# Places of the moving tiles and weight buffers modulo 512 bytes, and dense products in passes of 256 columns

## Chip, cores and metric

The kernel runs on one core of one Trainium2 chip. The metric is the device time of one execution in microseconds (us): the median of three runs, 2741.3 us before the change. All rows of profiles come from one profiled execution each.

## The reference

A trunk of two layers over 256 tokens of width 2048, float32. Layer 0 has differential attention, layer 1 a gated DeltaNet; each layer ends with a gated feed-forward with a short causal convolution (ConvFFN).

```python
for i in range(DEPTH):
    h = rms_norm(x, mixer_norm[i])
    if i % 2 == 0:
        x = x + diff_attention(h, w_qkv, ..., w_o, lambda_init)
    else:
        x = x + gated_deltanet(h, w_in, conv_w, a_log, dt_bias, norm_g, w_out)
    x = x + conv_ffn(rms_norm(x, ffn_norm[i]), ffn_w_up[i], ffn_conv_w[i], ffn_conv_b[i], ffn_w_down[i])

def conv_ffn(h, w_up, conv_w, conv_b, w_down):
    u = causal_dwconv(h @ w_up, conv_w) + conv_b
    val, gate = jnp.split(u, 2, axis=-1)
    return (jax.nn.silu(gate) * val) @ w_down
```

Nearly all of the arithmetic is in the dense products: q, k, v and w_o of the attention (2048 wide), w_up to 2 x 5504 and w_down back in each feed-forward, w_in, w_z and w_out of the DeltaNet.

## The kernel before

Activations lie transposed: features on the 128 partitions, the 256 tokens along the free axis. `x` is 16 tiles of 256 columns. `self.h` is 16 tiles of 128 x 2 x 256 in float32r; the first half of a tile is the high part of the normed activation, the second half the rest, so that the two add up to the float32 value (`norm_tile`). The feed-forward's own activations are kept in the same form in 43 tiles `ac`, the attention's in 16 tiles `ac`, the DeltaNet's in tiles `oc`.

Weights arrive in chunks of 512 KB: four tiles of 128 rows by 256 columns. `weights` loads one to `raw` (four buffers, SP's queue), ScalarE writes the high part `whi` (line 78) and VectorE the rest `wlo` (line 79), three buffers each.

`dense` makes a block of 256 output features in two PSUM banks, one for each 128. For each row tile k of the weights and each column tile c it issues three products: hi x hi, lo x hi, hi x lo. In the form with `fold` these are three passes of 256 columns into the first half of the bank (lines 107 to 109: a triple). Otherwise one pass of 512 columns takes both parts of the activation at once (line 112), and a pass of 256 columns adds the weight's rest to the second half of the bank (line 115: a pair); the halves are added after, in `merge` (lines 125 and 126) or `add_out` (line 235). Pairs are used for w_qk, w_o, w_gate, both w_up and both w_down but for the last block of the second; triples for w_in, w_out and that block. `dense_tok` (w_v and w_z) has the tokens on the partitions: there the weights are the moving operand, 512 columns wide, and slices of h are loaded into the array (lines 140 to 142).

The order is that of the program: attention, feed-forward, DeltaNet, feed-forward. Within a stage the blocks follow each other; small products of the attention and of the DeltaNet run as generators, one step after each chunk (`tick`). The numbers of passes, from the loops:

| stage | pairs | triples | passes of 512 alone |
|---|---|---|---|
| w_qk, w_gate | 512 + 16 | | |
| w_v, w_z | | | 384 + 768 |
| w_o | 256 | | |
| first w_up, w_down | 1376 + 688 | | |
| w_in, w_out | | 1024 + 512 | |
| second w_up, w_down | 1376 + 602 | 86 | |

Where a tile stands in a partition follows from the sizes of the tiles allocated before it. A tile of h or `ac` has 2048 bytes in each partition, a buffer of `whi` or `wlo` 4096, and the slice of 128 columns that one pass loads into the array 512.

Of the kernel before, what the change touches and what calls it, by code (L numbers as in the profile page):

```python
# [8 lines left out]
F32 = mybir.dt.float32  # L9
F32R = mybir.dt.float32r  # L10
AF = mybir.ActivationFunctionType
ALU = mybir.AluOpType
# [13 lines left out]
class Trunk:  # L26
    """Activations lie transposed, features on the partitions and the 256 tokens along the free axis.

    A float32 operand of a dense product is split into two float32r parts (hi + lo, exact), and
    the passes carry hi * hi, hi * lo and lo * hi; the parts of an activation lie side by side, so  # L30
    that one pass of a weight's hi takes both, and the two halves of the sum are added after. Work that follows a dense block and needs the
    tensor engine again runs as a generator in the background, a step after each chunk of weights.
    """

    def __init__(self, ctx, tc):
# [13 lines left out]
        self.h = [self.cp.tile([P, 2, T], F32R, tag=f"h{k}", name=f"h{k}") for k in range(KD)]  # L49
# [4 lines left out]
        nc.scalar.preload_act_table_set(LNEXP)  # L54

# [11 lines left out]
    def weights(self, ap):  # L67
        """A chunk [128, k, n] of weights, in two parts."""
        nc = self.nc
        nk, n = ap.shape[1:]  # L70

        def tile_(tag, dt, bufs):
            t = self.wp.tile([P, CK * T], dt, tag=tag, name=tag, bufs=bufs)
            return t[:, :nk * n].rearrange("p (k n) -> p k n", n=n)

        raw, hi, lo = tile_("raw", F32, 4), tile_("whi", F32R, 3), tile_("wlo", F32R, 3)
        nc.sync.dma_start(raw, ap)
        nc.scalar.copy(hi, raw)  # L78
        nc.vector.tensor_tensor(lo, raw, hi.bitcast(F32), ALU.subtract)  # L79
# [10 lines left out]
    def dense(self, w, kt, acts, tiles=2, fold=False, lead=0):  # L90
        """out^T of 128 * tiles features, a PSUM bank for each 128, in two halves to be added,
        or (fold) in one, which spares the vector engine the sum."""
        nc = self.nc
        ps = self.banks()
        for k0, nk in self.chunks(kt, CK, lead):
            hi, lo = self.weights(w[:, k0:k0 + nk, :])
            steps = [(k, c) for k in range(nk) for c in range(tiles)]
            if fold and k0 + nk == kt:
                steps = [(k, c) for c in range(tiles) for k in range(nk)]
            for k, c in steps:  # L100
# [3 lines left out]

                def sole():
                    o = ps[:, c, :T]
                    nc.tensor.matmul(o, hi[:, k, s], a[:, 0, :], start=first, stop=False)  # L107
                    nc.tensor.matmul(o, lo[:, k, s], a[:, 0, :], start=False, stop=False)  # L108
                    nc.tensor.matmul(o, hi[:, k, s], a[:, 1, :], start=False, stop=last)  # L109

                def one():
                    nc.tensor.matmul(ps[:, c, :], hi[:, k, s], a, start=first, stop=last)  # L112

                def two():
                    nc.tensor.matmul(ps[:, c, T:], lo[:, k, s], a[:, 0, :], start=False, stop=False)  # L115

                for f in ((sole,) if fold else (one, two) if first else (two, one)):
                    f()
# [3 lines left out]
    def merge(self, ps, u):  # L122
        """The two halves of a dense block, added and divided by the rms of the tokens."""
        nc = self.nc
        nc.scalar.copy(u, ps[:, :, T:])
        nc.vector.tensor_tensor(u, ps[:, :, :T], u, ALU.add)
# [22 lines left out]
    def norm_tile(self, k, gcol):  # L149
        """One tile of x * gain, split; 1 / rms is applied after the products."""  # L150
# [19 lines left out]
    def norm_stat(self, wait=1):  # L170
        """1 / rms of each token, over all partitions and as columns."""
# [22 lines left out]
    def lnexp(self, inst):  # L194
        """After inst, the activations within run from the table set that has both functions."""
# [4 lines left out]
    def conv(self, out, u, taps, bias):  # L200
        """Causal depthwise convolution along the tokens."""
# [10 lines left out]
    def rsqrt(self, out, ps, n):  # L212
        """(ps / n + eps) ** -0.5"""
# [4 lines left out]
    def split(self, out, a):  # L218
        """Two float32r parts of a, out[:, 0] + out[:, 1] = a."""
# [3 lines left out]
    def total(self, out, parts):  # L223
        """Sums over the partitions of tiles, in two parts each, on every partition."""
# [6 lines left out]
    def add_out(self, blk, ps, done, fold=False):  # L231
# [9 lines left out]
    def project(self, w, kt, acts, done, final=False):  # L241
        """x += a projection; with final, the last block is left a tile at a time."""
# [3 lines left out]
        if final:  # L246
            ps = self.dense(w[n - 1], kt, acts, fold=True)
# [5 lines left out]
    def ffn(self, w_up, w_down, nj, cols_ap, done, final=False):  # L253
        """cols_ap: taps (3) and bias, each for the values and the gates, a column for each tile."""
        nc = self.nc
        self.spawn(self.norm_stat())
        with self.tc.tile_pool(name="fp", bufs=1) as fp:
            cols = fp.tile([P, 4, 2, nj], F32, tag="fcols", name="fcols")
            nc.scalar.dma_start(cols, cols_ap)
            acts = []  # L260
            for j in range(nj):
                ps = self.dense(w_up[j], KD, self.h_acts)
                c = []
                u = fp.tile([P, 2, T], F32, tag="u", name="u", bufs=2)
                self.merge(ps, u)
# [8 lines left out]
                ac = fp.tile([P, 2, T], F32R, tag=f"ac{j}", name="ac")  # L274
# [4 lines left out]
    def attention(self, w_qk, w_v, w_o, nh, dist_ap, ident_ap, qg, kg, lvec, sub, start, done, lambda_init):  # L279
        """qg, kg, lvec (4 columns), sub (2 columns): per-partition columns."""  # L280
        nc, mp = self.nc, self.mp
        with self.tc.tile_pool(name="at", bufs=1) as at:
# [5 lines left out]
            dist = at.tile([P, 384], F32, tag="dist", name="dist")  # L288
# [44 lines left out]
            def weigh(h, qn, kn, go, aT):  # L333
                """The differential attention weights of a head, keys on the partitions."""
# [77 lines left out]
    def gdn(self, w_gate, w_in, w_z, w_out, nb, hb, gate_ap, const_ap, hot_ap, conv_col, ng, done):  # L412
        """nb batches of hb query/key heads, each with two value heads; 128 wide, all of them.

        const_ap: identity, mask of the decays, upper triangle of ones.
        All 256 tokens are one chunk: u = (I + strict(K K^T . D) beta)^-1 v, o = (Q K^T . D) beta u, with
        D_ij = exp(G_i - G_j) for i >= j, beta within the exponent. Matrices lie transposed, as
        [second half of the keys: 128 queries | first half: 256 queries].
        """
# [5 lines left out]
        with tc.tile_pool(name="gd", bufs=1) as gd:  # L425
            self.spawn(self.norm_stat())
            con = gd.tile([P, 384], F32, tag="con", name="con")
# [18 lines left out]
            def lin(ps):  # L446
                u = gd.tile([P, 2, T], F32, tag="u", name="u", bufs=2)
                nc.vector.tensor_tensor(u, ps[:, :, :T], self.rstd.unsqueeze(1).to_broadcast([P, 2, T]), ALU.mult)
# [9 lines left out]
            def keys(hq, c, cc, b0, res):  # L458
                """Decayed K K^T and Q K^T of the two value heads of a query/key head."""
# [52 lines left out]
            def invert(cc, lqs, inv):  # L512
                """Inverses of the unit lower triangular 32x32 blocks on the diagonal, one in a partition."""
# [23 lines left out]
            def levels(TT, Ta, lts, ttc, tcc, m0):  # L537
                """Transposes of the inverses of the 128x128 blocks, from those of the 32x32 ones."""
# [54 lines left out]
            def group(gi, gr, lqs, inv, vt, ready, zts, acts):  # L593
                """Outputs of the value heads of a group, on their way to the last projection."""
# [67 lines left out]
            def out(b, acts):  # L662
                for blk in range(KD // 2):
                    ps = self.dense(w_out[b * (KD // 2) + blk], 2 * hb, lambda k: self.await_(acts, k), fold=True)
# [244 lines left out]
```

## Time and profile before

| | |
|---|---|
| runs | 2741.3 us median of 3 (2741.16 to 2741.84) |
| profiled execution | span 2741.9 us, 44249 instructions, clock 0.999 |
| PE busy | 2727.6 us, 17526 passes |
| PEld busy | 2433.3 us |
| DVE busy | 1920.3 us |
| ACT busy | 1498.2 us |
| DMA | 481 MB, mean 175 GB/s |

PE is TensorE's products, PEld its weight loads (they overlap the products), DVE is VectorE, ACT ScalarE, POOL GpSimd, SP the engine that issues the transfers. A pass's duration in a row is from its start until its result is written; the next pass starts long before that, so the rate of the engine is read from the starts of passes that follow each other.

### The profile page before, as it was taken

To read this page: it belongs to the slowest core of one execution; us is meant where nothing else is said; L and a number is where in the kernel's file an instruction comes from. 1 tells how busy PE (TensorE), PEld (TensorE's weight loads), DVE (VectorE), ACT (ScalarE), POOL (GpSimd) and SP (SyncE) were. 2 spreads that over 40 slices of the span, in tenths; PEclk is the share of its full clock that TensorE was granted. 3 is DMA by queue.
4 is the path that set the end of the run, shared out by engine and by line. 5 is a ranking of instruction groups with operands and counts; after the bars stand their busy time and mean duration, and the time that the engine had idled before them with its cause. 6 is when DMAs were issued, how large, how long until landed. Compare 5 with 4: busy or idle time off the path is not lost.

```text
span 2741.9 us, 44249 instructions
## 1 busy us (share of the span) xinstructions
PE 2727.6 (99%) x17526; PEld 2433.3 (89%) x17526; DVE 1920.3 (70%) x2845; ACT 1498.2 (55%) x2094; POOL 117.0 (4%) x220
## 2 busy tenths in 40 slices
PE   8999999999999999999999999999999999999999
PEld 7888888888888888989989989989998888888888
DVE  7776577777777555679687687688677777776444
ACT  6665555555555444574564664574555555554333
POOL 0000000000000000022011011021000000000000
PEclk9999999999999999999999999999999999999999
DMA  6555565555555665655354454454455555556664
GB/s 210 170 166 173 156 193 186 185 186 188 187 185 188 187 187 185 187 158 180 116 164 168 131 170 146 154 167 157 152 185 187 186 186 186 188 187 194 191 195 151
DMA packets 135359, 481.00 MB, mean 175 GB/s; under 512 B 15344, under 2 KB 18416, under 8 KB 135152
## 3 DMA queue, kind: packets, MB, share of 16 engines
q1 hardware_dynamic: 134000, 475.57, 55.0%
q8 instruction: 137, 2.24, 0.3%
q10 hardware_dynamic: 1152, 2.61, 0.3%
q14 instruction: 70, 0.57, 0.1%
HBM read 476.03 MB, written 2.10 MB: 174 GB/s over the span
## 4 chain that ended last, share of the span: by engine, by line
PE 99%; DMA 0%; DVE 0%; ACT 0%; SPq 0%; issue 0%; DVEq 0%
PE ps L112 41%; PE ps L115 21%; PE ps L108 7%; PE ps L107 7%; PE ps L109 7%; PE ps L141 3%; PE ps L140 3%; PE ps L142 3%; PE mp L610 2%; PE mp L228 1%; PE mp L498 1%; PE mp L553 0%; PE mp L562 0%; PE mp L475 0%; PE mp L580 0%; PE mp L574 0%
## 5 line engine op out<-in xcount | busy, mean ns | idle before, releaser
L79 DVE TENSOR_TENSOR wlo<-raw,whi 128x1024 fp32r<-128x1024 f32 (+2 forms) x909 | 1107.1, 1218 | 571.5 <-ACT whi L78 568.7
L78 ACT CAST whi<-raw 128x1024 fp32r<-128x1024 f32 (+2 forms) x909 | 947.0, 1042 | 775.0 <-PE ps L112 475.5
L112 PE MATMUL ps<-h,whi 128*128 128x512 f32 x3280 | 1155.2, 398 | 6.1 <-DVE h L155 6.1
L115 PE MATMUL ps<-h,wlo 128*128 128x256 f32 x3280 | 908.4, 282 | 4.1 <-DVE wlo L79 4.1
L112 PEld LDWEIGHTS ps<-h,whi 128*128 128x128 f32 x3280 | 611.3, 188 | 147.7 <-DVE h L155 6.1
L115 PEld LDWEIGHTS ps<-h,wlo 128*128 128x128 f32 x3280 | 617.5, 188 | 14.1 <-DVE wlo L79 4.7
L112 PE MATMUL ps<-ac,whi 128*128 128x512 f32 x1546 | 543.5, 396 | 0.2 <-DVE x L235 0.2
L115 PE MATMUL ps<-ac,wlo 128*128 128x256 f32 x1546 | 430.2, 281 | 0.0
L112 PEld LDWEIGHTS ps<-ac,whi 128*128 128x128 f32 x1546 | 289.1, 188 | 68.7 <-ACT whi L78 0.5
L115 PEld LDWEIGHTS ps<-ac,wlo 128*128 128x128 f32 x1546 | 290.3, 188 | 2.0
L108 PE MATMUL ps<-h,wlo 128*128 128x256 f32 x1024 | 287.5, 281 | 0.0
L107 PE MATMUL ps<-h,whi 128*128 128x256 f32 x1024 | 286.1, 280 | 0.0
L109 PE MATMUL ps<-h,whi 128*128 128x256 f32 x1024 | 285.9, 279 | 0.0
L108 PEld LDWEIGHTS ps<-h,wlo 128*128 128x128 f32 x1024 | 193.7, 189 | 2.1
L107 PEld LDWEIGHTS ps<-h,whi 128*128 128x128 f32 x1024 | 193.1, 189 | 1.5 <-ACT whi L78 0.2
L109 PEld LDWEIGHTS ps<-h,whi 128*128 128x128 f32 x1024 | 193.2, 189 | 1.0
L140 PE MATMUL ps<-whi,h 128*128 128x512 f32 x384 | 151.5, 395 | 0.0
L141 PE MATMUL ps<-wlo,h 128*128 128x512 f32 x384 | 151.2, 394 | 0.0
L142 PE MATMUL ps<-whi,h 128*128 128x512 f32 x384 | 150.8, 393 | 0.0
L108 PE MATMUL ps<-oc,wlo 128*128 128x256 f32 x512 | 144.2, 282 | 0.0
L107 PE MATMUL ps<-oc,whi 128*128 128x256 f32 x512 | 144.1, 282 | 0.0
L109 PE MATMUL ps<-oc,whi 128*128 128x256 f32 x512 | 143.9, 281 | 0.0
(215 smaller groups left out, 2710.6 us busy)
## 6 DMA issues: line engine op xcount, KB each, us to landing
raw<-w_up SPq DMA_DIRECT2D x344, 512.0 KB, 4.4
raw<-w_down SPq DMA_DIRECT2D x160, 512.0 KB, 3.5
raw<-w_in SPq DMA_DIRECT2D x128, 512.0 KB, 4.4
raw<-w_z SPq DMA_DIRECT2D x64, 512.0 KB, 3.7
raw<-w_out SPq DMA_DIRECT2D x64, 512.0 KB, 3.8
raw<-w_qk SPq DMA_DIRECT2D x63, 512.0 KB, 3.9
raw<-w_v SPq DMA_DIRECT2D x32, 512.0 KB, 3.5
raw<-w_o SPq DMA_DIRECT2D x32, 512.0 KB, 4.7
```

Of the source, the lines that this page charges most:

```text
L78: nc.scalar.copy(hi, raw)
L79: nc.vector.tensor_tensor(lo, raw, hi.bitcast(F32), ALU.subtract)
L107: nc.tensor.matmul(o, hi[:, k, s], a[:, 0, :], start=first, stop=False)
L108: nc.tensor.matmul(o, lo[:, k, s], a[:, 0, :], start=False, stop=False)
L109: nc.tensor.matmul(o, hi[:, k, s], a[:, 1, :], start=False, stop=last)
L112: nc.tensor.matmul(ps[:, c, :], hi[:, k, s], a, start=first, stop=last)
L115: nc.tensor.matmul(ps[:, c, T:], lo[:, k, s], a[:, 0, :], start=False, stop=False)
L140: nc.tensor.matmul(ps[:, c, :], ah, hi[:, k, :], start=first, stop=False)
L141: nc.tensor.matmul(ps[:, c, :], ah, lo[:, k, :], start=False, stop=False)
L142: nc.tensor.matmul(ps[:, c, :], al, hi[:, k, :], start=False, stop=last)
L228: last = self.nc.tensor.matmul(out, self.onesr, p[:, j], start=i + j == 0, stop=i + j == n)
L610: nc.tensor.matmul(p[:, v, :], l(v), r[:, v, :], start=i == 0, stop=i == len(terms) - 1)
```

## The change

Four things, in one diff. First, each tile of h and of the feed-forward's `ac` gets 8 spare columns (32 bytes), so that the next one starts 32 bytes further modulo 512 (`staggered`); `fcols` and `dist` get spare columns as well, which moves what is allocated after them. Second, the three buffers of `whi` and of `wlo` become six tiles with names of their own, with 0, 32, 16 and 16, 56, 0 spare columns; they still take turns in threes. Third, `dense` uses triples everywhere but in the second feed-forward's w_up (`halves`), where the pass of 512 columns stays and the weight's rest now goes to the first half of the bank, after it. `merge` and `add_out` lose the sum of halves where there are none. Fourth, in the last chunk of a block all of column tile 0 is done before column tile 1, in every block and not only in folded ones. Comments are removed too.

```diff
-        self.h = [self.cp.tile([P, 2, T], F32R, tag=f"h{k}", name=f"h{k}") for k in range(KD)]
+        self.h = [self.staggered(self.cp, f"h{k}", f"h{k}") for k in range(KD)]
+        self.nth = 0
...
+    def staggered(self, pool, tag, name):
+        return pool.tile([P, 2 * T + 8], F32R, tag=tag, name=name)[:, :2 * T].rearrange("p (i t) -> p i t", i=2)
...
-        def tile_(tag, dt, bufs):
-            t = self.wp.tile([P, CK * T], dt, tag=tag, name=tag, bufs=bufs)
+        def tile_(tag, dt, bufs, spare=0):
+            t = self.wp.tile([P, CK * T + spare], dt, tag=tag, name=tag, bufs=bufs)
             return t[:, :nk * n].rearrange("p (k n) -> p k n", n=n)
-        raw, hi, lo = tile_("raw", F32, 4), tile_("whi", F32R, 3), tile_("wlo", F32R, 3)
+        b = self.nth % 3
+        self.nth += 1
+        raw = tile_("raw", F32, 4)
+        hi, lo = tile_(f"whi{b}", F32R, 1, (0, 32, 16)[b]), tile_(f"wlo{b}", F32R, 1, (16, 56, 0)[b])
...
-    def dense(self, w, kt, acts, tiles=2, fold=False, lead=0):
+    def dense(self, w, kt, acts, tiles=2, lead=0, halves=False):
...
-            if fold and k0 + nk == kt:
+            if k0 + nk == kt:
                 steps = [(k, c) for c in range(tiles) for k in range(nk)]
...
-                for f in ((sole,) if fold else (one, two) if first else (two, one)):
-                    f()
+                o = ps[:, c, :T]
+                if halves:
+                    nc.tensor.matmul(ps[:, c, :], hi[:, k, s], a, start=first, stop=last)
+                    nc.tensor.matmul(o, lo[:, k, s], a[:, 0, :], start=False, stop=False, skip_group_check=True)
+                    continue
+                nc.tensor.matmul(o, hi[:, k, s], a[:, 0, :], start=first, stop=False)
+                nc.tensor.matmul(o, lo[:, k, s], a[:, 0, :], start=False, stop=False)
+                nc.tensor.matmul(o, hi[:, k, s], a[:, 1, :], start=False, stop=last)
...
     def merge(self, ps, u):
-        nc.scalar.copy(u, ps[:, :, T:])
-        nc.vector.tensor_tensor(u, ps[:, :, :T], u, ALU.add)
-        nc.vector.tensor_tensor(u, u, self.rstd.unsqueeze(1).to_broadcast([P, 2, T]), ALU.mult)
+        self.nc.vector.tensor_tensor(u, ps[:, :, :T], self.rstd.unsqueeze(1).to_broadcast([P, 2, T]), ALU.mult)
...
-        for i in range(1 if fold else 2):
-            self.nc.vector.tensor_tensor(x, ps[:, :, i * T:(i + 1) * T], x, ALU.add)
+        self.nc.vector.tensor_tensor(x, ps[:, :, :T], x, ALU.add)
...
-            cols = fp.tile([P, 4, 2, nj], F32, tag="fcols", name="fcols")
+            cols = fp.tile([P, 8 * nj + 64], F32, tag="fcols", name="fcols")[:, :8 * nj]
+            cols = cols.rearrange("p (t h j) -> p t h j", t=4, h=2)
...
-                ps = self.dense(w_up[j], KD, self.h_acts)
+                ps = self.dense(w_up[j], KD, self.h_acts, halves=final)
...
-                ac = fp.tile([P, 2, T], F32R, tag=f"ac{j}", name="ac")
+                ac = self.staggered(fp, f"ac{j}", "ac")
...
-            dist = at.tile([P, 384], F32, tag="dist", name="dist")
+            dist = at.tile([P, 384 + 72], F32, tag="dist", name="dist")[:, :384]
```

More of the change, by code (lines that the diff above doesn't have):

```diff
@@ L103, in dense @@
                 s = slice(c * P, (c + 1) * P)
[L105 to L115, printed above, removed]
-                for f in ((sole,) if fold else (one, two) if first else (two, one)):
-                    f()
+                o = ps[:, c, :T]
+                if halves:
+                    nc.tensor.matmul(ps[:, c, :], hi[:, k, s], a, start=first, stop=last)
+                    nc.tensor.matmul(o, lo[:, k, s], a[:, 0, :], start=False, stop=False, skip_group_check=True)
[3 more added lines that the diff above has]
+                nc.tensor.matmul(o, hi[:, k, s], a[:, 1, :], start=False, stop=last)
             self.tick()
@@ L122, in merge @@
     def merge(self, ps, u):
-        nc = self.nc
-        nc.scalar.copy(u, ps[:, :, T:])
-        nc.vector.tensor_tensor(u, ps[:, :, :T], u, ALU.add)
-        nc.vector.tensor_tensor(u, u, self.rstd.unsqueeze(1).to_broadcast([P, 2, T]), ALU.mult)
+        self.nc.vector.tensor_tensor(u, ps[:, :, :T], self.rstd.unsqueeze(1).to_broadcast([P, 2, T]), ALU.mult)
     def dense_tok(self, w, kt, acts):
@@ L229, in total, with add_out @@
         return last
-    def add_out(self, blk, ps, done, fold=False):
+    def add_out(self, blk, ps, done):
         x = self.x[:, 2 * blk:2 * blk + 2, :]
-        for i in range(1 if fold else 2):
-            self.nc.vector.tensor_tensor(x, ps[:, :, i * T:(i + 1) * T], x, ALU.add)
+        self.nc.vector.tensor_tensor(x, ps[:, :, :T], x, ALU.add)
         if done:
@@ L246, in project @@
         if final:
-            ps = self.dense(w[n - 1], kt, acts, fold=True)
+            ps = self.dense(w[n - 1], kt, acts)
             for c in range(2):
@@ L261, in ffn @@
             for j in range(nj):
-                ps = self.dense(w_up[j], KD, self.h_acts)
+                ps = self.dense(w_up[j], KD, self.h_acts, halves=final)
                 c = []
                 u = fp.tile([P, 2, T], F32, tag="u", name="u", bufs=2)
-                self.merge(ps, u)
+                if final:
+                    nc.scalar.copy(u, ps[:, :, T:])
+                    nc.vector.tensor_tensor(u, ps[:, :, :T], u, ALU.add)
+                    nc.vector.tensor_tensor(u, u, self.rstd.unsqueeze(1).to_broadcast([P, 2, T]), ALU.mult)
+                else:
+                    self.merge(ps, u)
                 for half in range(2):
@@ L426, in gdn @@
             self.spawn(self.norm_stat())
-            con = gd.tile([P, 384], F32, tag="con", name="con")
+            con = gd.tile([P, 384], F32, tag="con", name="con")[:, :384]
             nc.sync.dma_start(con, const_ap)
@@ L447, in lin @@
                 u = gd.tile([P, 2, T], F32, tag="u", name="u", bufs=2)
-                nc.vector.tensor_tensor(u, ps[:, :, :T], self.rstd.unsqueeze(1).to_broadcast([P, 2, T]), ALU.mult)
+                self.merge(ps, u)
                 return u
@@ L663, in out @@
                 for blk in range(KD // 2):
-                    ps = self.dense(w_out[b * (KD // 2) + blk], 2 * hb, lambda k: self.await_(acts, k), fold=True)
-                    self.add_out(blk, ps, done if b == nb - 1 else None, True)
+                    ps = self.dense(w_out[b * (KD // 2) + blk], 2 * hb, lambda k: self.await_(acts, k))
+                    self.add_out(blk, ps, done if b == nb - 1 else None)
             pg = self.dense(w_gate, KD, self.h_acts, tiles=1)
@@ L679, in gdn @@
                         hq = heads[i]
-                        c = convs(lin(self.dense(w_in[hq * 2], KD, self.h_acts, fold=True)), (hq, nq + hq))
+                        c = convs(lin(self.dense(w_in[hq * 2], KD, self.h_acts)), (hq, nq + hq))
                         self.spawn(keys(hq, c, cc, 2 * i, lqs))
@@ L698, in gdn @@
                         hq = heads[i]
-                        c = convs(lin(self.dense(w_in[hq * 2 + 1], KD, self.h_acts, fold=True)),
+                        c = convs(lin(self.dense(w_in[hq * 2 + 1], KD, self.h_acts)),
                                   (2 * nq + 2 * hq, 2 * nq + 2 * hq + 1))
@@ L714, in gates @@
         lin = gd.tile([P, T], F32, tag="tmp", name="glin", bufs=1)
-        nc.scalar.copy(lin, pg[:, 0, T:])
-        nc.vector.tensor_tensor(lin, pg[:, 0, :T], lin, ALU.add)
-        nc.vector.tensor_tensor(lin, lin, self.rstd, ALU.mult)
+        nc.vector.tensor_tensor(lin, pg[:, 0, :T], self.rstd, ALU.mult)
         yield
```

## The prediction

> **What bounds the kernel now.** I read the page first: busy times, granted clock, chain of waits, costliest groups.
>
> ```profile
> span 2741.9 us, 44249 instructions
> PE 2727.6 (99%) x17526; PEld 2433.3 (89%) x17526; DVE 1920.3 (70%) x2845; ACT 1498.2 (55%) x2094; POOL 117.0 (4%) x220
> PEclk9999999999999999999999999999999999999999
> PE 99%; DMA 0%; DVE 0%; ACT 0%; SPq 0%; issue 0%; DVEq 0%
> L79 DVE TENSOR_TENSOR wlo<-raw,whi 128x1024 fp32r<-128x1024 f32 (+2 forms) x909 | 1107.1, 1218 | 571.5 <-ACT whi L78 568.7
> L78 ACT CAST whi<-raw 128x1024 fp32r<-128x1024 f32 (+2 forms) x909 | 947.0, 1042 | 775.0 <-PE ps L112 475.5
> L108 PE MATMUL ps<-h,wlo 128*128 128x256 f32 x1024 | 287.5, 281 | 0.0
> L107 PE MATMUL ps<-h,whi 128*128 128x256 f32 x1024 | 286.1, 280 | 0.0
> L109 PE MATMUL ps<-h,whi 128*128 128x256 f32 x1024 | 285.9, 279 | 0.0
> L140 PE MATMUL ps<-whi,h 128*128 128x512 f32 x384 | 151.5, 395 | 0.0
> L141 PE MATMUL ps<-wlo,h 128*128 128x512 f32 x384 | 151.2, 394 | 0.0
> L142 PE MATMUL ps<-whi,h 128*128 128x512 f32 x384 | 150.8, 393 | 0.0
> ```
>
> The reader is to see that TensorE is the whole chain, at full clock, with 14 us of idle time in 2742. So the time is the number of passes times the spacing of one pass to the next, and only a change of those two moves it. The durations in these rows are not spacings, since passes overlap; the spacing comes from the order in time. Two places in the stage of w_in, both the same three lines:
>
> ```profile
> 1149.77 0.28 PE L107 MATMUL ps<-h,whi 128*128 128x256 f32 x1
> 1150.71 0.28 PE L109 MATMUL ps<-h,whi 128*128 128x256 f32 x1
> ...
> 1183.19 0.28 PE L108 MATMUL ps<-h,wlo 128*128 128x256 f32 x1
> 1183.67 0.28 PE L109 MATMUL ps<-h,whi 128*128 128x256 f32 x1
> ...
> 1261.74 0.28 PE L109 MATMUL ps<-h,whi 128*128 128x256 f32 x1
> 1262.76 0.28 PE L109 MATMUL ps<-h,whi 128*128 128x256 f32 x1
> ```
>
> There are 8 passes between the first two rows, 117.5 ns each; 4 between the next two, just after a small product had broken in, 120 ns each; 9 between the last two, 113.3 ns each. Same instructions, same shapes, no idle time, three speeds. The duration of a pass tells which it ran at:
>
> ```profile
> L107 PE MATMUL ps<-h,whi x1024: 276/276/415, 1143.7 to 1896.7; 128*128 128x256 f32 x171
> L107 PE MATMUL ps<-oc,whi x512: 276/281/388, 1462.1 to 2008.1; 128*128 128x256 f32 x171
> L107 PE MATMUL ps<-ac,whi x86: 281/281/281, 2707.5 to 2737.6; 128*128 128x256 f32 x86
> L112 PE MATMUL ps<-h,whi x3280: 388/397/795, 6.1 to 2494.7; 128*128 128x512 f32 x193
> L140 PE MATMUL ps<-whi,h x384: 388/394/503, 214.0 to 1858.3; 128*128 128x512 f32 x192
> L498 PE MATMUL mp<-cv x64: 379/380/382, 1189.2 to 1828.1; 128*128 128x256 f32 x64
> L654 PE MATMUL mp<-con,zt x64: 270/272/273, 1345.5 to 1962.8; 128*128 128x128 f32 x64
> ```
>
> (Columns: least/median/longest ns.) 276 goes with a spacing of 113.3, 281 with 117.5: the duration is the spacing and 163 ns of latency. So passes of 256 columns come in two kinds, fast 276 and slow 281; passes of 512 columns between 388 (spacing 225) and 397 (234), the slow one being the median of line 112. The last two rows are plain float32 products, whose columns take twice the time each: a stream as long as one of 512 float32r columns has 380, one as long as 256 has 272. Those are the shortest for their length, 217 and 109 spacing. Something therefore costs the dense passes 4 to 9 ns per 256 columns.
>
> What it is not: the feed-forward stage keeps one rate whatever else runs.
>
> ```profile
> 430.00:780.00 350.00, 350.00 (x1985) 304.39 (x1985) 259.43 (x374) 198.63 (x280) 0.00 (x0) 1.00 0.59 187
> 780.00:1130.00 350.00, 350.00 (x1985) 304.23 (x1984) 208.68 (x255) 164.16 (x209) 0.00 (x0) 1.00 0.59 185
> ```
>
> (Stretches: length, then busy time of PE, PEld, DVE, ACT, POOL, clock, DMA share, GB/s.) DVE is busy 259 us in the one and 209 in the other, ACT 199 and 164, and PE starts 1985 passes in both: 352.7 ns for a pair of lines 112 and 115. A cost that other engines' traffic made would differ. What is left is PE's own two streams from SBUF, the moving tile and the next weights. Does their place matter? In the kernel before each tile of h and of the feed-forward is 2048 bytes, each weight buffer 4096, each weight slice 512, so all starts of a kind are equal modulo 512: by the allocation h at 160, weights at 480, the feed-forward's and the GDN's products at 416, and the attention's products, which feed w_o, at 384. The stage of w_o runs the same code as w_down:
>
> ```profile
> L112 PE MATMUL ps<-ac,whi 128*128 128x512 f32 x81 | 28.0, 392 | 0.0
> L115 PE MATMUL ps<-ac,wlo 128*128 128x256 f32 x80 | 22.0, 280 | 0.0
> ```
>
> Means of 392 and 280 against 397 and 281: less 163 each that is 346 ns a pair where w_down takes 352.7. With the same lines, the one thing that I know to differ is the place of the tile. So place does seem to matter, by some 6 ns a pair.
>
> **The change part by part.**
>
> *Passes.* Pairs (512 and 256 columns) become triples of 256 in w_qk (512), w_gate (16), the first feed-forward (1376 up, 688 down) and the second's w_down (602): 3194, and 256 in w_o. The same 768 columns, one weight load more. A triple at the slow kind is 3 x 117.5 = 352.5, at the fast 340.0, against 352.7 now. So the conversion alone is worth between nothing and 12.7 ns each, by which kind the passes settle in. If each pass cost more than 117.6 it loses.
>
> *Places.* Each tile of h and of the feed-forward's products is 2080 bytes, so h goes through 160, 192, ... modulo 512, all sixteen steps of 32. By the sizes, and if the allocator keeps its order, the weights come to 480, 32, 384 (hi) and 480, 160, 448 (lo). One relation no longer holds for a whole stage. No row shows a rotating place. The bounds per pass of 256 are 109 (the float32 row) and 120 (the rows after an interruption); I take 113.3, the fast kind, since it is the one measured for this very instruction, reached in two of the GDN's stages, and near the middle of the two ends. For 512 columns the ends are 217 and 234 and I take 225.
>
> *The sum.*
> - 3194 pairs: 352.7 to 340.0, 40.6 us.
> - 256 pairs of w_o: 346 to 340, 1.5 us.
> - w_in, 1024 triples: the means 281, 280, 279 to 276, 12.3 us; w_out, 512 triples with medians of 281 by its row, at most 512 x 3 x 5 = 7.7. Some of the means are passes held up by a small product of the GDN, which stay: I take half, 10.0 us.
> - the last 86 triples: 3 x 5 x 86 = 1.3 us.
> - 1376 pairs of the second w_up, which stay pairs: 352.7 to 225 + 113.3, 14 ns each, 19.8 us; bounds 0 and 1376 x (352.7 - 326) = 36.7.
> - 1152 passes of 512 columns in w_v and w_z: means 395, 394, 393 to 388, 384 x 18 ns = 6.9 us; bounds 0 and 384 x 42 = 16.
>
> Together 80.1 us. The span, 2741.9, and the runs' median, 2741.3, are the same within 0.6; the prediction is 2741.3 - 80.1 = 2661 us.
>
> *The other edits, at nothing, with their cover.*
>
> ```profile
> L126 DVE TENSOR_TENSOR u<-ps,u 128x512 f32<-128x512 f32 x86 | 59.5, 692 | 96.6 <-ACT u L125 96.6
> L125 ACT COPY u<-ps 128x512 f32<-128x512 f32 x86 | 50.4, 586 | 150.9 <-PE ps L112 150.7
> ```
>
> The sum of two halves goes in the first feed-forward and the attention (692 ns of DVE and 586 of ACT a block; half of these 86 stay in the second w_up). DVE is not on the chain, so that is no gain. Its cover: a chunk of weights costs ACT 1042 and DVE 1218, and PE 24 passes, 2.72 us at 113.3 ns; both engines keep slack. The last chunk of every block is done column tile by column tile, so the first bank is done half a chunk earlier; nobody waits for it. Transfers must go from 187 to 194 GB/s; SP's queue and its four raw buffers are unchanged, three weight buffers rotate as before. Should a chunk arrive late, the next is whi's cast on ACT.
>
> *A rule against the change.* The w_o row above says that place counts. The Trainium skill, page "TensorE: Matmul & The Clock Gate", section "Step-by-step: what each phase is for", says the opposite: the array has two independent SBUF read ports, so loading the next weights takes no bandwidth from the running product. By that rule the pads do nothing and only the conversion counts: the third rival below, 2722 us. The trace so far disagrees in w_o, with its 6 ns, though in one stage only.
>
> **The rivals.**
>
> 1. *The loss goes altogether.* Every dense pass runs as the float32 rows: 272 for 276, 380 for 388. Beyond the forecast 3 x 4 = 12 ns on 5072 triples (60.9 us), 8 on 1152 long passes (9.2), 12 on 1376 pairs (16.5): 86.6 us more, 2574 us. For it: the float32 rows have it in the same kernel. Against: no dense row has anything under 276 or 388, at any of the places shown.
> 2. *Slower: the streams never settle.* The place moves after every six passes. After an interruption the passes took 120 ns for some four passes before they fell to 113.3. If they never fall, each triple is 360: 3194 x 7.3 = 23.3, 256 x 14 = 3.6, and w_in and w_out, at 117.5 a pass with the means shown, 4608 x 2.5 = 11.5: 38.4 us more, 2780 us. It decides from 117.6 ns a pass on. Against: the interruption moves the time of the streams, not their place, and the rows fall back within six passes.
> 3. *Place does nothing.* The converted passes then mix as w_in (median 276) and w_out (281) do, 278.5 or 115.5 ns spacing: 3194 x 6 = 19.2 us less, w_o no gain, 2722 us. Against: w_o.
> 4. *All settle at the slow kind*, as the last 86 triples do, at 281 from first to last: 3194 x 0.2, nothing. About 2741 us.
>
> **How the numbers follow.** Forecast 45%, rival 1 22%, rival 2 13%, rival 3 11%, rival 4 9%. About 0.2% (5.5 us) is what a measurement of this kernel tells from no change. Faster: forecast, rivals 1 and 3, 78%; same: rival 4, 9%; slower: rival 2, 13%. The range for 8 in 10 goes from 2580, which leaves out the end of rival 1, to 2742, which takes in rival 4 and leaves out rival 2. The forecast's own range is 2630 to 2700: long passes and the second w_up at their bounds, w_in and w_out with no gain.
>
> **What would show it.** Passes of 256 columns in the first feed-forward at medians of 276 or less, 1.02 us for nine; the second w_up under 345 ns a pair; long passes of w_z near 388; PE still 99% of the chain and its idle time near 14 us. Wrong: medians of 281 or more (rivals 2 and 4), of 272 (rival 1), stages that differ only as they did before (rival 3), or idle time of PE that ends with whi or wlo, which would make the supply of weights the bound.

## The result, and the profile after

The kernel after takes 2766.8 us (median of 4 runs, 2765.8 to 2767.5) where the kernel before took 2741.6 in the same session: ratio 1.0089, 95% interval 1.0077 to 1.0102. It is slower by 25 us. The prediction said 2661 and faster; it was wrong, and outside its range.

The page after: its first lines, its chain of waits, and four of its groups of dense passes (busy us, mean ns of one, idle time before):

```profile
span 2765.3 us, 51003 instructions
PE 2750.7 (99%) x20976; PEld 2614.3 (95%) x20976; DVE 1884.8 (68%) x2762; ACT 1476.6 (53%) x2037; POOL 118.7 (4%) x220
PEclk9999999999999999999999999999999999999999
PE 99%; DVE 0%; DMA 0%; ACT 0%; issue 0%; ACTq 0%; DVEq 0%; SPq 0%
L116 PE MATMUL ps<-h,whi 128*128 128x256 f32 x2928 | 826.7, 283 | 9.0 <-ACT h L151 6.6
L113 PE MATMUL ps<-h,whi 128*128 128x512 f32 x1376 | 482.3, 395 | 0.0
L114 PE MATMUL ps<-h,wlo 128*128 128x256 f32 x1376 | 385.8, 280 | 0.0
L116 PE MATMUL ps<-oc,whi 128*128 128x256 f32 x512 | 146.2, 286 | 0.0
```

The bound is what it was: TensorE is 99% of the chain, at full clock, idle for 14.6 us against 14.3. No supply of weights, no VectorE, no queue has taken over. So the 23.4 us by which the span grew lie in the spacing of the passes. Busy PE and its passes in five stretches, first of the kernel before (first w_up and second w_up), then of the kernel after (first w_up, first w_down, second w_up); the columns are as in the prediction:

```profile
420.00:880.00 460.00, 460.00 (x2609) 400.08 (x2608) 342.66 (x495) 262.79 (x370) 0.00 (x0) 1.00 0.59 186
2020.00:2480.00 460.00, 460.00 (x2609) 400.05 (x2608) 340.96 (x491) 262.69 (x369) 0.00 (x0) 1.00 0.59 186
```

```profile
420.00:880.00 460.00, 460.00 (x3889) 459.95 (x3888) 318.09 (x448) 241.55 (x325) 0.00 (x0) 1.00 0.59 186
910.00:1140.00 230.00, 230.00 (x1948) 230.00 (x1948) 114.27 (x118) 95.57 (x111) 0.00 (x0) 1.00 0.58 183
2050.00:2500.00 450.00, 450.00 (x2570) 393.50 (x2569) 339.02 (x482) 259.19 (x364) 0.00 (x0) 1.00 0.60 188
```

Length over passes is the spacing (two or three passes that the edges cut are counted in, so 0.1% is not to be read from it). Before: 352.6 ns a pair. After: 118.3 ns a pass and 355 a triple in the first w_up (118.1 and 354 in w_down), where 113.3 and 340 were forecast; 350 a pair in the second w_up, where 338 was. The lines of w_in and w_out, whose rows of before stand in the prediction (medians 276 and 281):

```profile
L116 PE MATMUL ps<-h,whi x1028: 274/281/415, 1149.7 to 1920.0; 128*128 128x256 f32 x172
L116 PE MATMUL ps<-oc,whi x512: 277/281/420, 1476.7 to 2033.9; 128*128 128x256 f32 x171
```

The median of w_in has risen from 276 to 281: the stage that already had the fast kind of pass lost it. By stages, each from the first start of its passes to that of the next stage's (us, worked out from the starts in the traces; in the kernel after, the first pass of w_v stands ahead of the last 23 of w_qk, and these are counted to w_qk):

| | w_qk | w_v | w_o | first up | first down | DeltaNet | second up | second down |
|---|---|---|---|---|---|---|---|---|
| before | 207.9 | 100.8 | 92.9 | 486.5 | 243.0 | 871.2 | 486.5 | 242.9 |
| after | 208.2 | 101.8 | 95.7 | 489.3 | 243.9 | 888.8 | 483.0 | 243.8 |

17.6 of the 23.4 us are in the DeltaNet; w_o and the first w_up have 2.8 each, w_v 1.0, both w_down 0.9; only the second w_up gains, 3.5. Within the DeltaNet, from the start of each pass to that of the next, w_in and w_gate take 11.8 us more, w_out 5.2, w_z 1.3, and the small products 0.6 less.

### The profile page after: what moved, and what is told of

It is laid out like the page before. It is cut to its first block, busy times and chain, and to the rows that moved or that the text cites. A ratio compares the mean times of both kernels' runs of the same rounds, so it can differ in the third digit from the quotient of the medians.

```text
span 2765.3 us, 51003 instructions
## 1 busy us (share of the span) xinstructions
PE 2750.7 (99%) x20976; PEld 2614.3 (95%) x20976; DVE 1884.8 (68%) x2762; ACT 1476.6 (53%) x2037; POOL 118.7 (4%) x220
## 4 chain that ended last, share of the span: by engine, by line
PE 99%; DVE 0%; DMA 0%; ACT 0%; issue 0%; ACTq 0%; DVEq 0%; SPq 0%
PE ps L117 22%; PE ps L116 22%; PE ps L118 22%; PE ps L113 12%; PE ps L114 6%; PE ps L137 3%; PE ps L138 3%; PE ps L139 3%; PE mp L612 2%; PE mp L225 1%; PE mp L500 1%; PE mp L555 0%; PE mp L564 0%; PE mp L477 0%; PE mp L582 0%; PE mp L576 0%
## 5 line engine op out<-in xcount | busy, mean ns | idle before, releaser
L116 PE MATMUL ps<-h,whi 128*128 128x256 f32 x2928 | 826.7, 283 | 9.0 <-ACT h L151 6.6
L117 PE MATMUL ps<-h,wlo 128*128 128x256 f32 x2928 | 827.6, 283 | 0.4 <-DVE wlo L86 0.4
L118 PE MATMUL ps<-h,whi 128*128 128x256 f32 x2928 | 824.6, 282 | 0.0
L116 PEld LDWEIGHTS ps<-h,whi 128*128 128x128 f32 x2928 | 553.0, 189 | 11.6 <-ACT h L151 6.5
L118 PEld LDWEIGHTS ps<-h,whi 128*128 128x128 f32 x2928 | 553.7, 189 | 1.4
L113 PE MATMUL ps<-h,whi 128*128 128x512 f32 x1376 | 482.3, 395 | 0.0
L116 PE MATMUL ps<-ac,whi 128*128 128x256 f32 x1632 | 458.4, 281 | 1.0 <-DVE x L231 1.0
L117 PE MATMUL ps<-ac,wlo 128*128 128x256 f32 x1632 | 458.3, 281 | 0.0
L118 PE MATMUL ps<-ac,whi 128*128 128x256 f32 x1632 | 457.5, 280 | 0.0
L114 PE MATMUL ps<-h,wlo 128*128 128x256 f32 x1376 | 385.8, 280 | 0.0
L113 PEld LDWEIGHTS ps<-h,whi 128*128 128x128 f32 x1376 | 258.4, 188 | 60.4
L116 PEld LDWEIGHTS ps<-ac,whi 128*128 128x128 f32 x1632 | 307.3, 188 | 1.2 <-issue 1.1
L117 PEld LDWEIGHTS ps<-ac,wlo 128*128 128x128 f32 x1632 | 307.5, 188 | 0.0
L118 PEld LDWEIGHTS ps<-ac,whi 128*128 128x128 f32 x1632 | 307.0, 188 | 0.0
L116 PE MATMUL ps<-oc,whi 128*128 128x256 f32 x512 | 146.2, 286 | 0.0
```

## The experiments

### The passes without the places, and the places without the passes

First kernel: the change with every tile at its old size. Second: the kernel before with the change's sizes.

```diff
# passes alone (from after)
-pool.tile([P, 2 * T + 8], ...)          +pool.tile([P, 2 * T + 0], ...)
-(0, 32, 16)[b] ... (16, 56, 0)[b]       +(0, 0, 0)[b] ... (0, 0, 0)[b]
-8 * nj + 64, 384 + 72                   +8 * nj + 0, 384 + 0
# places alone (from before): all spare columns as after, pairs and triples as before
```

> The changed kernel with every tile and buffer back at its old size, so that all places modulo 512 are as before; triples where the change has them. Theory A (passes lock into a fast kind only while the places of moving tile and weights hold still; the rotation of places cost the GDN its fast passes): w_in and w_out keep their median of 276 and 281, the GDN's stage keeps about 871 us, the time is at or under before: 2742 if the converted passes settle at 281, 2700 if they settle at 276. Theory B (the extra weight load of a triple is what costs): the GDN keeps 871 us but the first feed-forward is as slow as in the changed kernel or slower, 355 ns a triple, about 2748 to 2752 us.

> The kernel before with the change's places alone: spare columns in h, ac, whi, wlo, fcols and dist; pairs and triples as before. Theory A: the GDN loses what the changed kernel lost, 871 to 888 us, the feed-forwards' pairs gain the 2 to 3 ns each that the second w_up gained, 4268 pairs, 8 to 13 us: 2745 to 2752 us. Theory B: the GDN's triples are not touched by places, 871 us, and the pairs gain: 2730 us.

Passes alone: ten runs in two groups, 2716.0 to 2717.8 (four) and 2742.8 to 2745.2 (six); ratio 0.9967 (0.9935 to 1.0000). Places alone: 2748.3, 1.0020 (1.0011 to 1.0029). So places make the loss, and the passes by themselves are worth either nothing or some 26 us, and which of the two differs from run to run. The profiled execution of passes alone, with a time of 2744.6, is one of the slow group; first w_up and first w_down, and a line of w_in:

```profile
420.00:880.00 460.00, 460.00 (x3908) 460.00 (x3908) 318.97 (x450) 241.96 (x327) 0.00 (x0) 1.00 0.62 186
900.00:1130.00 230.00, 230.00 (x1955) 230.00 (x1954) 115.11 (x119) 95.20 (x111) 0.00 (x0) 1.00 0.63 184
L116 PE MATMUL ps<-h,whi x1028: 276/276/388, 1139.8 to 1896.9; 128*128 128x256 f32 x172
```

117.7 ns a pass: the slow kind of the prediction, from end to end. w_in keeps its median of 276, and the DeltaNet takes 873.1 us, near the 871.2 of before. Places alone, pairs in first and second w_up:

```profile
430.00:880.00 450.00, 450.00 (x2573) 393.34 (x2572) 335.50 (x483) 257.53 (x364) 0.00 (x0) 1.00 0.61 188
2050.00:2480.00 430.00, 430.00 (x2459) 375.89 (x2458) 320.02 (x459) 244.13 (x345) 0.00 (x0) 1.00 0.61 188
```

350 ns a pair, less than before: by stages the two feed-forwards gain 12 us. But its DeltaNet takes 886.8 us, 15.6 more, and w_o, whose pairs stood at another place, 2.6 more. Moving the places is good for the pairs of the feed-forwards and bad for triples, and the change made triples of most pairs.

### Half of the places each

The change with only the weights at six places, and with only h and `ac` 32 bytes further each (the spare columns of `fcols` and `dist` stay in both).

> The changed kernel with h and ac back at 2048 bytes a tile, the six weight places kept. The relation then holds for a chunk of 24 passes, not for 6. Theory A: the passes have time to settle inside a chunk, so medians under those of the changed kernel, 276 to 280: 2700 to 2755 us. Rival (any mixture of places costs the same average, 118 ns a pass, whatever its period): 2767 us.

> The changed kernel with all weight buffers at 4096 bytes, so at one place modulo 512, and h and ac rotating by 32 bytes a tile. The relation changes every 6 passes, in equal steps. Theory A: as the changed kernel, the passes never settle, 2760 to 2772 us. Rival (it is the six weight places that upset, since whi and wlo no longer stand alike): 2700 to 2742 us.

Weights alone: 2750.5, 1.0032 (1.0019 to 1.0045). Tiles of h and `ac` alone: 2758.1, 1.0059 (1.0042 to 1.0076). The first w_up and a line of w_in, first of the one, then of the other:

```profile
430.00:880.00 450.00, 450.00 (x3862) 450.00 (x3862) 313.95 (x443) 237.83 (x321) 0.00 (x0) 1.00 0.60 189
L116 PE MATMUL ps<-h,whi x1006: 274/278/387, 1150.3 to 1904.4; 128*128 128x256 f32 x168
```

```profile
430.00:880.00 450.00, 450.00 (x3811) 450.00 (x3811) 310.75 (x436) 235.25 (x318) 0.00 (x0) 1.00 0.62 186
L116 PE MATMUL ps<-h,whi x1024: 274/281/390, 1149.8 to 1914.7; 128*128 128x256 f32 x171
```

116.5 and 118.1 ns a pass; the DeltaNet takes 880.7 and 883.5 us. Either half loses fast passes of w_in, the first fewer. So it isn't the own place of one operand alone that counts, and a look at both together followed.

### The distance between the two operands, measured by itself

The passes-alone kernel with a stretch of products ahead of its work (its own time says nothing): runs of 24 passes of 256 float32r columns with a product of 32 x 32 between runs, each pass loading other weights, with the weights' place minus the moving tile's place as the only thing that changes from run to run. Below, distance means this difference.

```diff
+def at(rel, m, i):
+    a = 512 + m + rel // 4 + 128 * (i % 8)
+    return sc[:, a:a + P]
+def short(rel, n, m=0):
+    p = self.mp()
+    for i in range(n):
+        nc.tensor.matmul(p[:, :T], at(rel, m, i), sc[:, m:m + T], start=i == 0, stop=i == n - 1)
+    done(p)
...
+short(0, 200)
+for rel in range(0, 512, 16):
+    for _ in range(4):
+        short(rel, 24)
```

> The kernel of passes_only (places of before, triples) with a bench ahead of it: passes of 256 float32r columns from one fixed place, the weights of each at a chosen distance modulo 512 (every 16 bytes, then every 4), 24 passes at a time with one tiny product between; then the same with 512 columns, with weight loads of 64 and of 32 columns, with the distance turning every 1, 2, 6, 12 or 24 passes, with two banks in turn, and runs of 300 passes. Theory C (the pass loses to the next weight load, both reading SBUF): loads of 64 and 32 columns bring the spacing from 113 to 118 ns down towards 109; the distance sets which spacing a steady run takes; turning distances give about 118. Rival D (the loss is the moving stream's own or PSUM's): narrower loads change nothing, 113 to 118 at every distance. The bench adds some 1.1 ms, so the time says nothing.

The durations of line 85 (least/median/longest) in the stretches of distances 0, 48, 64, 80 and 320 bytes, then in the runs of 300 passes at 0 and at 320:

```profile
L85 PE MATMUL mp<-bsc x93: 278/283/387, 31.8 to 43.9; 128*128 128x256 f32 x93
L85 PE MATMUL mp<-bsc x90: 278/281/396, 70.3 to 81.9; 128*128 128x256 f32 x90
L85 PE MATMUL mp<-bsc x96: 276/276/383, 82.9 to 94.9; 128*128 128x256 f32 x96
L85 PE MATMUL mp<-bsc x95: 278/281/386, 95.5 to 107.8; 128*128 128x256 f32 x95
L85 PE MATMUL mp<-bsc x94: 276/276/383, 288.3 to 299.9; 128*128 128x256 f32 x94
L85 PE MATMUL mp<-bsc x253: 283/283/283, 1124.7 to 1155.0; 128*128 128x256 f32 x127
L85 PE MATMUL mp<-bsc x267: 276/276/276, 1199.8 to 1229.9; 128*128 128x256 f32 x134
```

Same instruction, same data, and in the last two stretches no other engine at work: 276 at distances 64 and 320, 281 to 283 at the three others, and in those stretches, without one exception, 283 at distance 0 (120.0 ns of spacing) and 276 at 320 (113.3). Of the 32 distances in steps of 16 bytes, only 64 and 320 have 113.3 ns, in all eight of their runs; the others lie between 116.7 and 120.6 (means of a run behind its first pass, from the starts in the trace), and the pattern repeats after 256 bytes. (In steps of 4 bytes, 52 has 113.3 as well; 8 and 12 have 115.6 to 116.5.) Moving both tiles together by 16 to 64 bytes leaves 0 at 118.1 to 119.9 and 320 at 113.3 to 117.8. A distance that turns, every pass or every 24, gives 116.7 to 118.5; the mean of the sixteen fixed distances is 118.1. Where it turns every 24 passes, the 24 at distance 64 have 117.8, though a run that starts there has 113.3. Passes of 512 columns go another way: 227.7 to 228.9 ns at 0, 192 and their like, 232.4 to 234.3 elsewhere, 233.5 at 64. Two PSUM banks in turn change nothing. Loading 64 or 32 columns of weights for 128 does not take the loss away: 113.3 to 118.6 over the four distances tried, at 64 and 320 mostly more than with 128, though at 0 with 64 columns less, 113.7 to 114.5 for 119.5. In each run the weights of a pass and of the next stand alike modulo 256, so whether it is the one's place or the other's that counts is not told apart.

Now the places of the prediction can be read again. Before, h stood at 160 and the weights at 480: distance 320, which is 64 modulo 256. `ac` of the feed-forward and `oc` stood at 416: distance 64. The attention's `ac` at 384: distance 96. The kernel before stood at the one fast distance of sixteen in w_in, w_out and both feed-forwards, and the change moved it through all of them. In the feed-forward that distance was no help: the passes of 512 columns in its pairs took 234.5 ns, near their 233.5 above, and those of 256 between them 118.5, not the fast kind (from the starts). w_o had its better pairs, 229.7 and 117.7 ns, at distance 96; the measurement by itself has 234.2 for 512 columns there, so it does not explain w_o, and pairs were not measured by themselves.

In the kernel with only the weights moved, by the sizes, both parts of a chunk in the first buffer stand at distance 64 from h, those of the second at 128 and 0, of the third at 224 and 32 (modulo 256). Three chunks that follow each other in its first w_up:

```profile
L117 PE MATMUL ps<-h,wlo x7: 276/276/276, 579.2 to 581.3; 128*128 128x256 f32 x7
L117 PE MATMUL ps<-h,wlo x7: 280/282/283, 581.9 to 584.1; 128*128 128x256 f32 x7
L117 PE MATMUL ps<-h,wlo x7: 277/280/281, 584.8 to 586.9; 128*128 128x256 f32 x7
```

Over the whole stage (from the starts) the chunks of the first buffer have 113.8 ns a pass in 55 of 57 cases, 114.3 and 118.1 in the other two, those of the second 117.9 and of the third 118.1 on average. That is the distance at work in the kernel itself, every third chunk. That both parts stand alike in the first buffer is not what does it: they do so in all buffers of the kernel with only h and `ac` moved, with its 118.1 ns.

### A fixed distance that is not 64, and one 256 bytes further

If any fixed place would do, the weights could stand anywhere. Passes alone, with one spare tile of 32 bytes ahead of the weight buffers, and `fcols` 480 bytes longer: h and `ac` stand at distances 352 and 96, which is 96 modulo 256, and `oc`, moved along with the weights, still at 64. Later the same with 256 bytes (without the longer `fcols`, with triples in the second w_up too, and the attention's `ac` at distance 64): h goes from 320 to 64, all `ac` and `oc` stand at 64.

```diff
+        self.wp.tile([P, 8], F32, tag="spare", name="spare", bufs=1)     # 32 bytes
+        self.wp.tile([P, 64], F32, tag="spare", name="spare", bufs=1)    # 256 bytes
```

> passes_only with the weight buffers 32 bytes further and the feed-forward's ac moved so that it stands 96 bytes before them modulo 512, h 352; all relations hold still. Theory A (still places lock, and the relation sets the speed): stages of h and ac run at other spacings than 113.3 or 117.5, by w_o of before some 115.5, the feed-forwards at 477 and 239 us: 2700 to 2720 us, and alike from run to run. Rival (any still relation locks into 113.3 or 117.5 by chance): 2716 to 2745 us and two groups of times, as passes_only had.

> The kernel without breaks, with the weight buffers 256 bytes further in a partition: weights minus moving tile 576 bytes, again 64 modulo 256, but 64 and not 320 modulo 512. Theory P (what counts is the distance modulo 256): the times of the kernel without breaks, 2690 to 2745 us, and passes of 113.3 ns in w_in. Rival Q (the distance modulo 512 or the weights' own place counts): as with the weights 32 bytes further, 2755 to 2765 us, no fast passes.

32 bytes: 2758.9, one group from 2758.7 to 2759.4, ratio 1.0063 (1.0046 to 1.0080). This fixed distance is as slow as rotating ones. 256 bytes: two groups again, 2712.8 to 2716.4 (six) and 2744.8 to 2746.3 (four), 0.9949 (0.9912 to 0.9987). The first w_up and w_in, first with 32 bytes, then with 256:

```profile
430.00:880.00 450.00, 450.00 (x3794) 450.00 (x3794) 309.09 (x433) 233.98 (x317) 0.00 (x0) 1.00 0.60 185
L117 PE MATMUL ps<-h,whi x1035: 276/280/393, 1149.8 to 1921.0; 128*128 128x256 f32 x173
```

```profile
430.00:860.00 430.00, 430.00 (x3796) 430.00 (x3796) 306.17 (x434) 233.88 (x316) 0.00 (x0) 1.00 0.64 194
L117 PE MATMUL ps<-h,whi x1027: 276/276/388, 1110.7 to 1866.6; 128*128 128x256 f32 x172
```

118.6 against 113.3 ns, 280 against 276. With 32 bytes w_in goes from 115.1 ns of passes alone to 117.9 (from the starts, interruptions left out), while w_out, at 64 in both, keeps 116.8. The distance counts modulo 256, in the kernel as in the measurement by itself.

### Two kinds of pass at the same place

What remained is the two groups. At distance 64 both 113.3 and 117.7 occur, and each holds until something comes between or the distance changes. Three kernels with all old places (and the attention's `ac` at 64) and triples everywhere: without breaks, with a product of 32 x 32 ahead of every block of the feed-forwards, and ahead of every eighth block of w_up and fourth of w_down.

```diff
+    def kick(self):
+        q = self.mp()
+        self.nc.tensor.matmul(q[:32, :32], self.ones[:32, :32], self.ones[:32, :32], start=True, stop=True)
...
+                if j % 8 == 0:
+                    self.kick()
                 ps = self.dense(w_up[j], KD, self.h_acts)
...
+            if kt == NJ and b % 4 == 0:
+                self.kick()
             self.add_out(b, self.dense(w[b], kt, acts), done)
```

> All places as in the kernel before (weights minus moving tile 320 bytes, which is 64 modulo 256, in every stage; the attention's products are moved to that place too), triples everywhere, the second w_up too. Theory E: at this place a pass has two steady kinds, 113.3 and 117.7 ns, and which one a stage falls in is chance, then kept. Then the runs fall in two or more groups between 2690 and 2745 us, the slow one near 2742, and in the profile each feed-forward is either about 487 us (slow kind) or 475 us (fast) for w_up as a whole. Rival F: triples are worth what pairs are, whatever happens: 2735 to 2745, one group.

> The same with a product of 32 x 32 x 32 ahead of every block of both feed-forwards (102 in all), whose result nobody reads. Theory E: a break lets the passes fall into the fast kind, and they stay in it: w_up 475 us, w_down 237 us and about 0.15 us for each break, 2700 us in all and one group of times. Rival F: the kind is set by something else, a break costs only itself: the groups of the kernel without breaks, 15 us higher.

> The same product ahead of every eighth block of w_up and every fourth of w_down only (16 in all). Theory E: 2685 to 2700 us, w_up at 475 us except for stretches of up to eight blocks before a break that happens to fall in the fast kind. Rival F: the groups of the kernel without breaks, 2 us higher.

Without breaks: 2714.3 to 2716.2 (four runs) and 2743.0 to 2745.5 (six), ratio 0.9965 (0.9930 to 1.0000). The profiled one is of the first group; first w_up and second w_up, the same lines at the same places:

```profile
420.00:860.00 440.00, 440.00 (x3885) 440.00 (x3884) 313.08 (x445) 240.79 (x325) 0.00 (x0) 1.00 0.64 194
2000.00:2430.00 430.00, 430.00 (x3653) 430.00 (x3653) 298.20 (x419) 225.19 (x305) 0.00 (x0) 1.00 0.60 187
```

113.3 ns through the one, 117.7 through the other. With a break every eighth block: 2691.6 (2691.2 to 2697.0), one group, ratio 0.9820 (0.9805 to 0.9835). Its profiled execution shows a break at work, in the first w_up; the stretch ahead of it, the one behind it, and the second w_up, then the break itself in order of time:

```profile
420.00:497.00 77.00, 77.00 (x656) 77.00 (x656) 53.77 (x76) 41.67 (x56) 0.00 (x0) 1.00 0.59 184
499.00:576.00 77.00, 77.00 (x682) 77.00 (x681) 54.86 (x78) 41.88 (x58) 0.00 (x0) 1.00 0.63 192
2000.00:2430.00 430.00, 430.00 (x3794) 429.66 (x3793) 307.27 (x436) 235.31 (x319) 0.00 (x0) 1.00 0.63 194
```

```profile
497.57 0.28 PE L118 MATMUL ps<-h,whi 128*128 128x256 f32 x1
497.78 0.24 PE L128 MATMUL mp<-ones 32*32 32x32 f32 x2
497.95 0.39 PE L116 MATMUL ps<-h,whi 128*128 128x256 f32 x1
498.17 0.28 PE L117 MATMUL ps<-h,wlo 128*128 128x256 f32 x1
```

117.7 ns a pass up to 497 us, 113.3 from then on, through four further breaks in w_up and two in w_down. The break meant for block 0 had been issued earlier, at 325.9 us in the stage of w_o, since nothing held it back. The passes there went from 117.8 to 113.3 behind it, and 7 us later a wait for VectorE turned them back to 117.8, which lasted into w_up:

```profile
325.95 0.24 PE L128 MATMUL mp<-ones 32*32 32x32 f32 x2
332.79 0.36 PE L116 MATMUL ps<-ac,whi 128*128 128x256 f32 x1 [1.06 <-DVE x L235]
```

In the kernel without breaks, and in that with 256 bytes, a wait of 0.98 us at the same point did the reverse, 117.8 to 113.3. So an interruption can go either way. Within the feed-forwards no break left the fast kind, in this profile or in that of a break every block. That one takes 2722.3 (2721.2 to 2723.5), ratio 0.9927 (0.9913 to 0.9942): fast all through, but a block with its break takes 11.25 us from one break to the next where its 96 passes take 10.88, so a break costs 0.37 us and not the 0.15 expected. 102 of them at 0.22 more are the 22 us by which the expectation was off.

### The breaks alone

> The kernel before, its pairs as they are, with the breaks of the last kernel but one ahead of every eighth block of w_up and every fourth of w_down. Theory E1: only triples have a fast kind at the place of 64 (its total of three passes, 340 ns, is reached; a pair's is 352.7 whatever breaks it): both feed-forwards stay at 486 and 243 us, 2743 to 2747 us. Rival E2: the breaks alone do it, and a pair too falls to about 340 ns: w_up near 470 us, 2690 to 2705 us, and the conversion was not needed.

> The kernel after, its rotating places as they are, with the same breaks. Theory E1: with places that change at every product there is no steady kind to fall into, so a break is worth nothing: w_up 489 us, 2767 to 2773 us. Rival E2: the breaks do it at any place, and the first feed-forward falls to 470 + 234 us: 2735 us or less.

The kernel before with these breaks: 2743.8 (2742.1 to 2745.0), 1.0006 (0.9996 to 1.0016). The kernel after with them: 2771.3 (2771.0 to 2771.8), 1.0107 (1.0092 to 1.0122). First w_up of the one and of the other:

```profile
430.00:880.00 450.00, 450.00 (x2554) 391.06 (x2553) 333.26 (x480) 255.59 (x360) 0.00 (x0) 1.00 0.60 186
```

```profile
430.00:880.00 450.00, 450.00 (x3800) 449.12 (x3799) 308.68 (x433) 234.09 (x317) 0.00 (x0) 1.00 0.62 185
```

352.4 ns a pair and 118.4 a pass, both untouched. In the kernel after, the breaks of the first feed-forward stand where they were meant, but for the one of block 0, which is in w_o. In the kernel before they do not: of the eight of the first feed-forward one is in w_o and seven at 425.5, 428.8 and 432.3 us, none later, and in the second it is much the same. So pairs were broken at a few moments only.

As far as these runs go, a feed-forward that is fast in all four runs took three things together: triples, the distance of 64, and a break that lets the passes fall into the fast kind. Without the break it differs from run to run; without the distance, or in pairs, no profile here shows a fast kind to fall into (for pairs, with few breaks). A break is not the only way in: in the kernel with only the weights moved, the change from another distance did it in nearly every chunk. The kernel with all three beats both, by 51 us and 75.

## Why the prediction was wrong

- **What bounds the kernel: right.** TensorE's spacing, at full clock, with 14 to 15 us idle before and after. The cover of the other edits held too, since that idle time did not grow.
- ***Places:* the step that failed.** "One relation no longer holds for a whole stage. [...] I take 113.3, the fast kind, since it is the one measured for this very instruction." The rows of 113.3 came from a stage whose distance is fixed at 64, and the measurement by itself shows that kind nowhere else on the grid of 16 bytes. A rotating distance gives about the mean of the sixteen, 118.1: 116.7 to 118.5 there and 118.3 in the kernel. I had written down the places of before, 160, 480 and 416, and did not take their differences, which are the same modulo 256 in w_in and w_out, where the fast passes were.
- **The reading of w_o: half right.** Place does count, by 6 ns a pair, as read. But I took from it that moving off the old place is good. That holds for the pairs of the feed-forwards (350 for 352.7 in the places-alone kernel) and not for triples, and the sum was mostly about triples.
- ***Passes,* −40.6 us forecast.** By "which kind the passes settle in", I wrote, the conversion is worth nothing to 12.7 ns each, and beyond 117.6 ns a pass it loses. With 118.3 it lost: 2.8 us in the first w_up, 0.9 in each w_down, 0.3 in w_qk. This is the largest miss, some 45 us. At the old places the same conversion gave either end of that range in the first feed-forward, depending on the run.
- **w_in and w_out, −10 us forecast:** +17.0 (with w_gate), most of the 17.6 by which the DeltaNet grew. It is the largest growth, and the same step: its fast passes were counted as a floor that place could only bring nearer.
- **w_o, −1.5:** +2.8. **Second w_up, −19.8:** −3.5; its passes of 512 and 256 columns average 350 ns a pair and not 338; no distance measured is fast for both lengths. **w_v and w_z, −6.9:** +1.0 and +1.3. In them slices of h are loaded and the weights move, so the distance before was 160 minus 480, which is 192 modulo 256, where 512 columns have 228.9 in the measurement by itself: 229.3 ns a pass (from the starts), and 232.0 after, where it rotates, for the 225 forecast. With 32 bytes the distance is 160, and w_z has 233.4, where the measurement by itself has 233.1 to 233.4. So they too stood at a fast place and were moved off it.
- **The rivals.** The first, the loss gone altogether, is excluded: no float32r pass kept a spacing under 113.3. The second, that the streams never settle, names what happened, with 118.3 ns where I took 120 for it, so 2767 and not 2780. I argued against it that the rows fall back after an interruption; they do so at distance 64 alone, and there not always. The third had place doing nothing: excluded by either half of the places, 8 and 16 us above the kernel before where no place moved gave about the same or 26 less. The fourth, all at the slow kind, is what the feed-forwards did in the profiled run of passes alone, one of its slow group, but not in the change.
- **The rule against the change.** The Trainium skill, page "TensorE: Matmul & The Clock Gate", section "Step-by-step: what each phase is for", has loading and running product on read ports that do not disturb each other. The runs differ: 283 and 276 ns for the same pass, by the distance of two tiles. Which part of the machine the two meet in is not shown; with 64 columns loaded the spacing at distance 0 fell from 119.5 to 114 ns and at 64 mostly rose from 113.3 to 118.5, so the loading has a part in it, but not by its mere amount.

Open: why 64 (and 52) and not another distance; why the passes have two steady kinds there; and what decides at an interruption which of them follows. In both profiles of triples everywhere without breaks the first feed-forward had the 113.3 of the end of w_o and the second the 117.8 of the end of w_out, so the kind is carried from stage to stage; whether this is what makes the two groups of times is argued, since no profile was taken of that kernel at 2743 to 2746 us.

## What to carry to other kernels

When rows of the same instruction show two speeds, work out what the fast place has in common before changing it: here one subtraction of two addresses would have shown that every fast row stood at the same distance. A fast row taken while something is fixed says nothing about what happens once that thing varies, and a mean over all settings is the safer estimate. When a kernel's runs fall in two groups, look for a stage that holds one of two rates from end to end, and for something cheap that moves it from one to the other.

## What the runs showed of the hardware

- The spacing of float32r passes of 256 columns depends on the loaded weights' place minus the moving tile's place in a partition, modulo 256 bytes: in runs that start at it 113.3 ns at 64, 116.7 to 120.6 at the other fifteen multiples of 16. For 512 columns it is 227.7 to 228.9 at 0 and 192, and 232.4 to 234.3 at the other multiples of 32, 64 among them.
- At 64 two kinds, 113.3 and 117.7 ns, each keep themselves up for hundreds of microseconds; a product of 32 x 32 between two passes can turn the slow into the fast, for 0.37 us; a wait of 1 us went both ways.
- No float32r pass of 256 columns had a steady spacing under 113.3 ns at any distance, with one bank or two, or with fewer columns loaded.
